# Splitting a weight tile's products into a high pass and a low pass, and mLSTM gates as products

## The chip, the cores and the metric

One Trainium2 chip, one of its cores. The metric is device time in microseconds (us) of one execution. The kernel before takes 2247.6 us (median of 3 runs, 2247.15 to 2248.94).

## What is computed

Four transformer layers over 256 tokens of width 1024, all in float32: two layers of a first kind (with 256 context tokens beside), then two of a second kind. Cut to what matters here:

```
# first kind: h and hc are adaptive RMS norms of x and ctx
q,k,v,gates,o,z, bq,bk,bv,bz, cu,cz, mg = split(h @ w_in)      # 1024 x 13328
h_a = mlstm(q, k, v, gates)          # forward and backward in time
y_a = rmsnorm(h_a) * sigmoid(o) * silu(z)
y_b = diff_attention(bq, bk, bv) * silu(bz);  y_c = fft2(cu) * silu(cz)
x  += gate * ((g_a*(y_a@w_a) + g_b*(y_b@w_b) + g_c*(y_c@w_c)) @ w_out)
# mlstm gates, per head and direction:
b = cumsum(log_sigmoid(f));  m = running max of (b_t - b_s + i_s), carried over chunks
decay weights = exp(b_t - b_s + i_s - m_t);  floor of the denominator = exp(-m_t)
# second kind
x += gt1 * ((sigmoid(ga)*swa(h)@w_o1 + sigmoid(gb)*moba(h)@w_o2) @ w_out)
x += gt2 * (relu(h2 @ w_up)**2 @ w_down)
```

Nearly all arithmetic is in the products with the weight matrices, each of 1024 rows or more.

## The kernel before

**Products in three parts.** A float32 number is split into a high part that TensorE multiplies in one pass (type fp32r) and a low part, the rest. A product of activations A = H + L with weights W = h + l is the sum of three matmuls: H with h, H with l and L with h. The activations' parts are made once, at each norm. The weights' parts are made tile by tile: a tile of 128 x 1024 numbers (512 KB) comes by DMA into a buffer `w`, ScalarE (ACT) copies it with rounding into another (the high part `h`), and VectorE (DVE) subtracts that from the raw tile into a third (the low part `l`). There are 9 such buffers, and some more for a while. Weights are moving data in the form `tok` (activations stand still), and stand still in the form `feat`.

**One program, written by a planner.** `Stream.execute` walks through all weight products in order (`gemm` lists them). For a product it visits pairs (q, o): weight tile q, output o, each output one PSUM bank `mm`. A tile of the usual width 512 holds two slices (`kq` = 2), so a visit is six matmuls: per slice the three parts one after another. After each three matmuls it calls `dma` (next tile's transfer), up to six steps of other work (`plan.side`: attention, norms, gates, evacuations of PSUM, written as generators), and `split` once. These decide where an instruction stands by the planner's own clock; on the chip each engine runs its instructions in the order written.

`split` makes a low part if one is owed and its high part is done by that clock, otherwise the next high part. `tile(i)` is what a visit calls first: it forces both parts of tile i into the program.

```
i = st["base"][q]
h, l = self.tile(i)
for j in range(kq):
    ...
    for m, (L, R, O) in enumerate(outs[o](h[:, s], l[:, s], kt, ps[o])):
        nc.tensor.matmul(O, L, R, ...)
```

The first tiles (`head`) and the last ones (`tail`) of some products are visited output by output, the others tile by tile.

**Gates.** `mlstm_gates` runs once in each of the two layers of the first kind, as side work. On rows (heads on partitions 0 to 3 forward, 32 to 35 backward; time along the row) it makes the sums `b` and maxima `cm`, the four chunks' carries (`TG`, `M`, `off`), and from these four rows per chunk, `R0` and R0 plus three offsets (`r1`, `r2`, `r3`), plus `F`. Five transposes per chunk of 128 time steps turn them into columns `cols`. The other work on TensorE, float32 matmuls and transposes into banks `p0` to `p3`, is written between the weight products; these groups are called p groups below.

Of the kernel before, what the change touches and what calls it, by code (L numbers as in the profile page):

```python
# [49 lines left out]
NSIDE, SLACK, MAXEV, LATE = 6, 1200.0, 4, 400  # L50
NP, NJ, MP = 3, 5, 2
# [284 lines left out]
class Stream:  # L336
# [64 lines left out]
    def build_seq(self):  # L401
# [29 lines left out]
        self.nd = self.ns = self.nl = self.pairs = 0  # L431
# [20 lines left out]
    def split(self, force=False):  # L452
# [5 lines left out]
        if self.nl < self.ns:  # L458
            i = self.gidx[self.nl]
            if force or plan.gate([self.h[i]]) <= plan.t[PE]:  # L460
                r, l = self.raw.pop(i), self.alloc(F32R)
                nc.vector.tensor_tensor(l, r, self.h[i].bitcast(F32), ALU.subtract)
                self.drop(r)
                self.l[i] = l
                self.nl += 1
                return True
        if self.ns < len(self.gidx) and self.pairs < (NP + MP if self.more else NP) and len(self.free) > 1 + self.ns - self.nl:
# [10 lines left out]
    def tile(self, i):  # L478

        plan = self.plan  # L480
        while i not in self.l:
# [10 lines left out]
        late = plan.gate([self.h[i], self.l[i]])  # L492
# [5 lines left out]
        return self.h[i], self.l[i]  # L498

    def execute(self):  # L500
        plan, nc = self.plan, self.nc
        self.build_seq()
        nout, evs = 0, []
# [15 lines left out]
        for st in self.prog:  # L519
# [14 lines left out]
            left = [no] * nq  # L534
            ps, seen = [None] * no, [0] * no
            for q, o in visits:
# [7 lines left out]
                h, l = self.tile(i)  # L544
# [6 lines left out]
                for j in range(kq):  # L551
                    kt = q * kq + j
                    s = slice(j * st["width"], (j + 1) * st["width"])
                    for m, (L, R, O) in enumerate(outs[o](h[:, s], l[:, s], kt, ps[o])):
                        nc.tensor.matmul(O, L, R, start=(kt == 0 and m == 0), stop=(seen[o] == st["nkt"] - 1 and m == 2))
                    seen[o] += 1
                    if j == kq - 1:
                        left[q] -= 1
                        if not left[q]:
                            self.drop(self.h.pop(i))  # L560
                            self.drop(self.l.pop(i))
                            self.pairs -= 1
                            if self.joint and self.joint[0] == i:
                                self.joint.pop(0)
                        if seen[o] == st["nkt"]:
                            evac(st["cb"], o, ps[o])
                    self.dma()
                    n = 0
                    while n < NSIDE and plan.side():
                        n += 1  # L570
                    self.split()
# [11 lines left out]
def _build(tc, a, out, es):  # L583
# [377 lines left out]
    def tok(act, t, c0=0, c1=512):  # L961
        ts = slice(128 * t, 128 * t + 128)

        def f(h, l, kt, ps):
            H, L = act(kt)
            O = ps[:, 0:c1 - c0]
            return [(H[:, ts], h[:, c0:c1], O), (H[:, ts], l[:, c0:c1], O), (L[:, ts], h[:, c0:c1], O)]
        return f

    def feat(view, f0, n):  # L970
        fs = slice(128 * f0, 128 * f0 + 128)

        def f(h, l, kt, ps):
# [4 lines left out]
            return [(h[:, fs], H, O), (h[:, fs], L, O), (l[:, fs], H, O)]  # L978
# [90 lines left out]
    def mlstm_gates(rowt, l, res):  # L1069

        def gen(lane):
            pre, lf, b, v, cm, r1, r2, r3 = (rowt[:, i, :] for i in range(8))
            R = slice(0, 36)
            nc.gpsimd.memset(rowt[R, 2, :], 0.0)
            nc.gpsimd.memset(rowt[R, 4:8, :], 0.0)
# [24 lines left out]
            TG = sm.tile([128, 2, 4], F32, name="TG", tag="TG")  # L1100
            nc.vector.memset(TG, 0.0)
            for i, arr in enumerate((b, cm)):
                fw = arr[0:4].rearrange("p (c n) -> p c n", n=128)[:, :, 127]
                bw = arr[32:36].rearrange("p (c n) -> p c n", n=128)[:, :, 0]
                nc.vector.tensor_copy(TG[0:4, i, 0:2], fw[:, 1:3])
                nc.vector.tensor_copy(TG[0:4, i, 2:4], fw[:, 0:4:3])
                for p, j in POS_B.items():
                    nc.vector.tensor_copy(TG[32:36, i, j:j + 1], bw[:, p:p + 1])
            M = sm.tile([128, 4], F32, name="M", tag="M")
            nc.vector.memset(M, 0.0)  # L1110
            for j in range(3):
                nc.vector.tensor_tensor(M[R, j + 1:j + 2], M[R, j:j + 1], TG[R, 1, j:j + 1], ALU.max)
                nc.vector.tensor_tensor(M[R, j + 1:j + 2], M[R, j + 1:j + 2], TG[R, 0, j:j + 1], ALU.add)
            off = sm.tile([128, 4, 4], F32, name="off", tag="off")
            nc.vector.tensor_copy(off[R, 1, 1:4], TG[R, 0, 0:3])
            nc.vector.tensor_tensor(off[R, 2, 2:4], off[R, 1, 2:4], TG[R, 0, 0:2], ALU.add)
            nc.vector.tensor_tensor(off[R, 3, 3:4], off[R, 2, 3:4], TG[R, 0, 0:1], ALU.add)
            yield [DVE]
            dirs = ((slice(0, 4), POS_F), (slice(32, 36), POS_B))
# [10 lines left out]
            rk = (R0, r1, r2, r3)  # L1130
            nc.gpsimd.memset(r1[R], 0.0)
            for k in (1, 2, 3):
                for rr, pos in dirs:
                    for p, j in pos.items():
                        if j >= k:
                            cs = slice(128 * p, 128 * p + 128)
# [291 lines left out]
    def layer1(l, X, norm, ada_next, begin_out, on_token):  # L1428
# [38 lines left out]
        def g_out(h, lo, kt, ps):  # L1467
            H, L = act(kt)
            return [(h, H, ps), (h, L, ps), (lo, H, ps)]
# [566 lines left out]
    def attend_items(kind, qk, vv, oo, scol, need):  # L2036


        def group(t, p0):
# [4 lines left out]
            def gen(lane):  # L2044
# [36 lines left out]
                for e in range(2):  # L2081
                    for i in range(hpb):
                        if i % 2 == 0 and (e or i):
                            yield []
# [401 lines left out]
```

## Time and profile before

| what | value |
|---|---|
| median of 3 runs | 2247.6 us |
| the profiled execution | 2247.62 us, of it the span 2245.5 us |
| TensorE (PE) busy | 2200.1 us, 98% of the span |
| VectorE (DVE), ScalarE (ACT) busy | 1485.1 us (66%), 1104.3 us (49%) |
| GpSimd (POOL) busy | 272.6 us (12%) |
| DMA | 359.73 MB, mean 160 GB/s |
| granted TensorE clock, mean | 0.997 |

The span runs from the first to the last instruction; 2.1 us of the execution lie around it. Matmuls overlap, and the profile models where each ends, so "busy" is an upper bound of work: a short wait that falls into the modelled end of the matmul before is not shown as idle time.

### The profile page before, as it was taken

What the parts mean: (1) busy time and instruction counts of PE and PEld (TensorE: products, weight loads), DVE (VectorE), ACT (ScalarE), POOL (GpSimd) and SP (SyncE); (2) the same over time, 40 slices, a digit from 0 to 9 for tenths busy, and PEclk for the clock granted to TensorE, in tenths of its full rate; (3) what the DMA queues carried; (4) which work ended last, traced back from release to release, by engine and by line L of the source; (5) the groups of instructions that cost most, each with busy time, mean ns of one, the idle gap of its engine ahead of it and who ended that gap; (6) DMA issues with size and microseconds to landing.
All of it is one profiled execution on the core that took longest, in us unless ns stands there. A gap on an engine that the chain in (4) does not pass through costs nothing. (4 is left out here: it accounts for less than half of the span.)

```text
span 2245.5 us, 33046 instructions
## 1 busy us (share of the span) xinstructions
PE 2200.1 (98%) x12312; PEld 1821.8 (81%) x12312; DVE 1485.1 (66%) x2778; ACT 1104.3 (49%) x2110; POOL 272.6 (12%) x467
## 2 busy tenths in 40 slices
PE   8999999999999999999999999999999999999999
PEld 6877888877777877877778888787898987798987
DVE  4667745457676744687886788677766656758554
ACT  4345422235565522344543466555855645666653
POOL 1013000014121000110200142003000002100000
PEclk9999999999999999999999999999999999999999
DMA  7443344353322453365675423464354564345454
GB/s 297 144 157 109 121 167 140 132 170 118 103 98 96 140 179 131 140 206 187 233 246 185 158 83 135 157 213 151 123 195 165 180 215 160 132 145 203 160 188 150
DMA packets 99905, 359.73 MB, mean 160 GB/s; under 512 B 11960, under 2 KB 12272, under 8 KB 99744
## 3 DMA queue, kind: packets, MB, share of 16 engines
q1 hardware_dynamic: 96192, 348.34, 45.3%
q0 software_dynamic: 3552, 9.28, 1.5%
q8 instruction: 97, 1.59, 0.3%
q14 instruction: 64, 0.52, 0.1%
HBM read 354.37 MB, written 3.20 MB: 159 GB/s over the span
## 5 line engine op out<-in xcount | busy, mean ns | idle before, releaser
L318 DVE TENSOR_TENSOR w<-w,w 128x1024 fp32r<-128x1024 f32 x451 | 551.5, 1223 | 394.0 <-ACT w L318 340.0
L318 ACT ACTIVATE w<-w 128x1024 fp32r<-128x1024 f32 x459 | 485.1, 1058 | 647.6 <-PE mm L318 595.4
L318 PE MATMUL mm<-h,w 128*128 128x256 f32 (+1 forms) x3280 | 665.5, 326 | 2.8 <-DVE w L318 2.3
L318 PE MATMUL mm<-w,h 128*128 128x512 f32 (+1 forms) x1972 | 597.7, 394 | 12.2 <-DVE w L318 9.0
L318 PEld LDWEIGHTS mm<-h,w 128*128 128x128 f32 x3280 | 479.6, 190 | 57.3 <-issue 9.6
L318 PEld LDWEIGHTS mm<-w,h 128*128 128x128 f32 x1972 | 357.2, 190 | 101.4 <-DVE w L318 15.5
L318 PE MATMUL mm<-w,s 128*128 128x512 f32 x1280 | 309.1, 392 | 1.2 <-DVE w L318 1.1
L318 PE MATMUL mm<-w,hl 128*128 128x512 f32 (+1 forms) x800 | 306.7, 383 | 0.0
L318 PEld LDWEIGHTS mm<-w,s 128*128 128x128 f32 x1280 | 238.4, 188 | 52.6 <-DVE w L318 3.2
L318 PE MATMUL mm<-hl,w 128*128 128x512 f32 (+1 forms) x656 | 245.8, 375 | 0.0
L318 PE MATMUL mm<-s,w 128*128 128x512 f32 (+1 forms) x960 | 182.2, 349 | 0.0
L318 PEld LDWEIGHTS mm<-w,hl 128*128 128x128 f32 x800 | 150.8, 189 | 29.9 <-DVE hl L318 0.2
L318 PEld LDWEIGHTS mm<-s,w 128*128 128x128 f32 x960 | 153.1, 190 | 23.5 <-issue 2.0
L318 DVE SCALAR_TENSOR_TENSOR acc<-w,stat,acc 128x512 f32<-128x512 f32 x192 | 143.8, 749 | 42.3 <-DMA w<-in_wada_dram 35.5
L318 PEld LDWEIGHTS mm<-hl,w 128*128 128x128 f32 x656 | 124.0, 189 | 18.7 <-issue 1.0
L318 ACT ACTIVATE s<-mm 128x512 f32<-128x512 f32 (+2 forms) x126 | 65.2, 521 | 62.8 <-PE mm L318 62.8
L318 POOL TENSOR_TENSOR qrs<-qrs,mhalf 128x8 f32<-128x8 f32 (+2 forms) x48 | 77.1, 1607 | 4.0
L318 PE MATMUL p<-s 64*128 64x256 f32 (+3 forms) x464 | 75.4, 389 | 1.4 <-DVE s L318 0.7
L318 POOL TENSOR_SCALAR ls<-ls 128x1 f32<-128x1 f32 x72 | 29.8, 414 | 344.5 <-ACT l1a L318 127.1
L318 PE MATMUL mm<-s,s 128*128 128x512 f32 x256 | 68.7, 390 | 0.0
L318 DVE TENSOR_REDUCE ls<-p 128x1 f32<-128x512 f32 (+1 forms) x96 | 52.8, 595 | 12.7 <-PE p L318 12.3
L318 ACT ACTIVATE s<-w 128x1024 fp32r<-128x1024 f32 x43 | 45.5, 1058 | 27.7 <-PE mm L318 21.0
(348 smaller groups left out, 2399.3 us busy)
## 6 DMA issues: line engine op xcount, KB each, us to landing
w<-in_win_dram SPq DMA_DIRECT2D x272, 512.0 KB, 3.3
w<-in_wada_dram SPq DMA_DIRECT2D x144, 512.0 KB, 3.5
w<-in_wmix_dram SPq DMA_DIRECT2D x64, 512.0 KB, 3.3
w<-in_wup_dram SPq DMA_DIRECT2D x64, 512.0 KB, 3.4
w<-in_wdn_dram SPq DMA_DIRECT2D x64, 512.0 KB, 3.2
w<-in_wo_dram SPq DMA_DIRECT2D x16, 512.0 KB, 3.2
w<-in_wout_dram SPq DMA_DIRECT2D x16, 512.0 KB, 3.5
s<-in_x_dram SPq DMA_DIRECT2D x4, 512.0 KB, 7.3
```

Of the source, the lines that this page charges most:

```text
L318: r = f(*a, **k)
```

## The change

Four edits.

1. **Order of products.** A visit is now a step (q, o, parts). For a middle tile of width 512 (neither the first nor the last tile of its product, nor in `head` or `tail`) the steps go part by part: high x high for all outputs, then the activations' low part with the weights' high part for all outputs, and last the weights' low part for all outputs. For the first tile of a product and for `head` tiles the order within an output is parts 0, 2, 1, where 2 is the weights' low part; for the others 0, 1, 2. Within a step the two slices of one part stand next to each other. (`tok` and `feat` list their parts so that number 2 always holds `l`.)
2. **Splits.** `tile(i)` asks for the high part only unless part 2 is due. `split` prefers a high part while fewer than `AHEAD` = 2 tiles from the current one on have theirs, and the new `pump` (after each three matmuls) may call `split` twice then.
3. **Gates.** Chunk carries are copied with fewer, strided instructions; the maximum with the carry is one instruction for all chunks (before 8). The rows r1, r2, r3 (12 instructions) go; instead four DVE products make offsets times the identity (`off`, 36x144), and two float32 matmuls per chunk add R0 (stationary) times the identity four times and ones times `off`. One transpose (for `F`) stays.
4. In the attention of the second kind of layers a `yield []` becomes `yield [ACT]`.

The core of the diff:

```diff
-        if self.nl < self.ns:
+        if self.nl < self.ns and not (self.ns < self.cur + AHEAD and self.split_high(force)):
...
+    def pump(self):
+        self.dma()
+        if self.ns < self.cur + AHEAD:
+            self.split()
+        n = 0
+        while n < NSIDE and self.plan.side():
+            n += 1
+        self.split()
...
-            visits = [(q, o) for o in range(no) for q in range(hd)]
-            visits += [(q, o) for q in range(hd, nq - tl) for o in range(no)]
-            visits += [(q, o) for o in range(no) for q in range(nq - tl, nq)]
+            early, late = (0, 2, 1), (0, 1, 2)
+            steps = [(q, o, early) for o in range(no) for q in range(hd)]
+            for q in range(hd, nq - tl):
+                if 0 < q < nq - 1 and kq == 2:
+                    steps += [(q, o, (p,)) for p in late for o in range(no)]
+                else:
+                    steps += [(q, o, late if q else early) for o in range(no)]
+            steps += [(q, o, late) for o in range(no) for q in range(nq - tl, nq)]
...
+                for p in parts:
+                    l = self.tile(i)[1] if p == 2 else None
...
+                        L, R, O = outs[o](h[:, s], None if l is None else l[:, s], kt, ps[o])[p]
+                        nc.tensor.matmul(O, L, R, start=(seen[o] == 0), stop=(seen[o] == total - 1))
...
-            for rr, pos in dirs:
-                for p, j in pos.items():
-                    cs = slice(128 * p, 128 * p + 128)
-                    nc.vector.tensor_scalar(cm[rr, cs], cm[rr, cs], M[rr, j:j + 1], None, ALU.max)
+            nc.vector.tensor_tensor(cm4, cm4, MP[R, :, 0:1].to_broadcast([36, 4, 128]), ALU.max)
...
-                            nc.vector.tensor_scalar(rk[k][rr, cs], R0[rr, cs], off[rr, k, j:j + 1], None, ALU.add)
...
+                nc.vector.tensor_tensor(off[:, c], ident[R, R].unsqueeze(1).to_broadcast([36, 4, 36]),
+                                        MP[R, c, 1:5].unsqueeze(2).to_broadcast([36, 4, 36]), ALU.mult)
...
-                for i, arr in enumerate((R0, r1, r2, r3, F)):
-                    nc.tensor.transpose(ps[:, 36 * i:36 * i + 36], arr[R, 128 * p:128 * p + 128], ident[R, R])
+                nc.tensor.matmul(pk, R0[R, cs], ident[R, R].unsqueeze(1).to_broadcast([36, 4, 36]), start=True, stop=False)
+                nc.tensor.matmul(pk, ones[R], off[:, p], start=False, stop=True)
+                nc.tensor.transpose(ps[:, 144:180], F[R, cs], ident[R, R])
```

First place: TensorE, the third tile (q = 2) of the second layer's product `gemm(W(3), ...)`, which makes the second half of the mLSTM values; four outputs. Before, its high part is `w2_8907` and its low part `w8_8944`; `h_7967` and `hl_7968` are the activations' high and low parts, and the `p` rows are the gates' transposes.

```order
L318 MATMUL mm_8889<-w4_8854,hl_7968 128x512
L318 MATMUL mm_8856<-w2_8907,h_7967 128x512
L318 MATMUL mm_8856<-w8_8944,h_7967 128x512
L318 MATMUL mm_8856<-w2_8907,hl_7968 128x512
L318 MATMUL mm_8856<-w2_8907,h_7967 128x512
L318 MATMUL mm_8856<-w8_8944,h_7967 128x512
L318 MATMUL mm_8856<-w2_8907,hl_7968 128x512
L318 MATMUL p2_8963<-cst_80,s3_8624 128x36 x5
L318 MATMUL mm_8869<-w2_8907,h_7967 128x512
L318 MATMUL mm_8869<-w8_8944,h_7967 128x512
```

In the changed program the same tile's high part is `w7_8863` and its low part `w2_8893`, the tile before it `w0_8808` and `w4_8817`:

```order
L319 MATMUL mm_8849<-w4_8817,h_7936 128x512 x2
L319 MATMUL p3_8911<-cst_80,s3_8592 128x144
L319 MATMUL p3_8911<-s3_8592,one_84 128x144
L319 MATMUL p3_8911<-cst_80,s3_8592 128x36
L319 MATMUL mm_8810<-w7_8863,h_7936 128x512 x2
L319 MATMUL mm_8827<-w7_8863,h_7936 128x512
L319 MATMUL p2_8922<-cst_80,s3_8592 128x144
L319 MATMUL p2_8922<-s3_8592,one_84 128x144
L319 MATMUL p2_8922<-cst_80,s3_8592 128x36
L319 MATMUL mm_8827<-w7_8863,h_7936 128x512
L319 MATMUL mm_8835<-w7_8863,h_7936 128x512 x2
L319 MATMUL mm_8849<-w7_8863,h_7936 128x512 x2
```

The low part was read by the tile's second matmul; now eight matmuls with the high part stand first, then eight with `hl_7936` and the high part, and only then those with `w2_8893`. Five transposes of 36 columns have become two products of 144 columns and one transpose.

Second place: VectorE, from the low part of that product's second tile (first row) to the low part of its third (`w8_8944`), with the gates between (`s3` holds the gates' rows, `M` and `off` the carries, `acc` an accumulation for the adaptive norms).

```order
L318 TENSOR_TENSOR w0_8867<-w3_8664,w4_8854 128x1024
L318 TENSOR_SCALAR acc_8866<-w7_8796,stat_88 128x512
L318 SCALAR_TENSOR_TENSOR acc_8866<-w7_8796,stat_88,acc_8866 128x512
L318 TENSOR_SCALAR s3_8624<-s3_8624,M_8839 4x128 x8
L318 TENSOR_TENSOR s3_8624<-s3_8624 36x512
L318 TENSOR_SCALAR s3_8624<-s3_8624 36x512
L318 TENSOR_SCALAR s3_8624<-s3_8624,off_8847 4x128 x12
L318 SCALAR_TENSOR_TENSOR acc_8866<-w7_8887,stat_88,acc_8866 128x512
L318 TENSOR_TENSOR w8_8944<-w5_8702,w2_8907 128x1024
```

The same stretch of VectorE in the changed program, up to the same tile's low part (`w2_8893`):

```order
L319 TENSOR_TENSOR w4_8817<-w8_8629,w0_8808 128x1024
L319 TENSOR_TENSOR modA1_8623<-p2_8815,col_82 128x4
L319 SCALAR_TENSOR_TENSOR modA1_8623<-modA1_8623,col_82 128x4
L319 TENSOR_SCALAR acc_8826<-w2_8761,stat_88 128x512
L319 SCALAR_TENSOR_TENSOR acc_8826<-w2_8761,stat_88,acc_8826 128x512
L319 COPY s3_8592<-s3_8592 4x10
L319 COPY s3_8592<-s3_8592 4x2x5 x3
L319 TENSOR_TENSOR s3_8592<-s3_8592 36x512 x2
L319 TENSOR_SCALAR s3_8592<-s3_8592 36x512
L319 TENSOR_TENSOR s3_8592<-cst_80,s3_8592 36x144 x4
L319 SCALAR_TENSOR_TENSOR acc_8826<-w2_8840,stat_88,acc_8826 128x512 x2
L319 TENSOR_TENSOR w2_8893<-w6_8670,w7_8863 128x1024
```

The 8 and the 12 instructions on 4x128 have gone; four copies, one maximum over 36x512 and four products of 36x144 stand in their place.

## Rows read from the trace of the kernel before

**Rows 1.** The page: span, busiest engine, and the granted clock in 40 slices.
```profile
span 2245.5 us, 33046 instructions
...
PE 2200.1 (98%) x12312; PEld 1821.8 (81%) x12312; DVE 1485.1 (66%) x2778; ACT 1104.3 (49%) x2110; POOL 272.6 (12%) x467
...
PEclk9999999999999999999999999999999999999999
```
**Rows 2.** Waits of PE: total us, times, longest.
```profile
PE mm L318 <- DVE w L318: 12.4, 14, 1.6
...
PE mm L318 <- ACT h L318: 2.7, 3, 1.2
PE mm L318 <- DVE h L318: 2.7, 4, 1.0
...
PE p L318 <- DVE qr L318: 1.7, 2, 1.4
```
**Rows 3.** Timeline of PE, 1017 to 1024 us: start, us, instruction, idle before.
```profile
1019.08 0.39 PE L318 MATMUL mm<-w,hl 128*128 128x512 f32 x1
1019.31 0.39 PE L318 MATMUL mm<-w,h 128*128 128x512 f32 x1
1021.27 0.50 PE L318 MATMUL mm<-w,h 128*128 128x512 f32 x1 [1.58 <-DVE w L318]
1021.62 0.40 PE L318 MATMUL mm<-w,hl 128*128 128x512 f32 x1
...
1022.65 0.50 PE L318 MATMUL p<-cst,s 36*128 36x36 f32 x5
1023.08 0.73 PE L318 MATMUL mm<-w,h 128*128 128x512 f32 x2
```
**Rows 4.** Timeline of DVE, 1008 to 1021.5 us.
```profile
1013.36 1.87 DVE L318 TENSOR_SCALAR s<-s,M 4x128 f32<-4x128 f32 x8
1015.27 0.68 DVE L318 TENSOR_TENSOR s<-s 36x512 f32<-36x512 f32 x1
...
1016.40 2.90 DVE L318 TENSOR_SCALAR s<-s,off 4x128 f32<-4x128 f32 x12
1019.33 0.75 DVE L318 SCALAR_TENSOR_TENSOR acc<-w,stat,acc 128x512 f32<-128x512 f32 x1
1020.00 1.22 DVE L318 TENSOR_TENSOR w<-w,w 128x1024 fp32r<-128x1024 f32 x1
```
**Rows 5.** Timelines of PE at 957.5, 1975, 31 and 1947.5 us.
```profile
959.48 0.50 PE L318 MATMUL mm<-w,h 128*128 128x512 f32 x1 [1.08 <-DVE w L318]
...
1975.98 1.21 PE L318 MATMUL mm<-h,w 128*128 128x256 f32 x8 [1.02 <-DVE w L318]
...
31.67 0.50 PE L318 MATMUL mm<-w,h 128*128 128x512 f32 x1 [0.43 <-DVE w L318]
...
1948.31 0.86 PE L318 MATMUL mm<-h,w 128*128 128x256 f32 x5 [0.47 <-DVE w L318]
```
**Rows 6.** Timeline of PE, 1936.5 to 1943.5 us.
```profile
1937.66 0.63 PE L318 MATMUL p<-cst,qr 128*128 128x128 f32 x4 [1.36 <-DVE qr L318]
1938.05 0.47 PE L318 MATMUL mm<-w,h 128*128 128x512 f32 x1
1940.04 3.91 PE L318 MATMUL mm<-w,h 128*128 128x512 f32 x9 [1.51 <-DVE w L318]
```
**Rows 7.** Windows: us, PE, PEld, DVE, ACT, POOL busy (count), granted clock, DMA.
```profile
1936.00:1939.50 3.50, 1.16 (x7) 0.58 (x5) 3.46 (x7) 3.04 (x10) 1.64 (x1) 1.00 0.42 152
1939.50:1942.90 3.40, 2.87 (x7) 2.30 (x8) 3.40 (x7) 1.28 (x4) 0.00 (x0) 0.63 0.00 0
```
**Rows 8.** The page, groups: busy us, mean ns of one, idle before and releaser.
```profile
L318 DVE TENSOR_TENSOR w<-w,w 128x1024 fp32r<-128x1024 f32 x451 | 551.5, 1223 | 394.0 <-ACT w L318 340.0
L318 ACT ACTIVATE w<-w 128x1024 fp32r<-128x1024 f32 x459 | 485.1, 1058 | 647.6 <-PE mm L318 595.4
```
**Rows 9.** Groups of PE by form: the small float32 products (two records each) and transposes.
```profile
L318 PE MATMUL p<-s,l0b 128*128 128x256 f32 x64 | 15.4, 381 | 0.0
...
L318 PE MATMUL p<-s,l2b 128*128 128x128 f32 x96 | 12.9, 277 | 0.2 <-ACT l2b L318 0.2
...
L318 PE MATMUL p<-cst,s 36*128 36x36 f32 x40 | 4.0, 231 | 0.0
```
**Rows 10.** The page, DMA issues: count, size, us from issue to landing.
```profile
w<-in_win_dram SPq DMA_DIRECT2D x272, 512.0 KB, 3.3
```

More of the change, by code (lines that the diff above doesn't have):

```diff
@@ L476, in split, with high, tile @@
         return False
-    def tile(self, i):
+    def high(self, i):
+        return self.tile(i, False)[0]
+    def tile(self, i, low=True):
         plan = self.plan
-        while i not in self.l:
+        while i not in (self.l if low else self.h):
             self.dma()
@@ L491, in tile @@
                 plan.side(force=True)
-        late = plan.gate([self.h[i], self.l[i]])
+        late = plan.gate([self.h[i], self.l[i]] if low else [self.h[i]])
         while late > plan.t[PE] + LATE:
@@ L502, in execute @@
         self.build_seq()
-        nout, evs = 0, []
+        nout, evs, since = 0, [], 0
         def evac(cb, o, ps):
@@ L543, in execute @@
                 i = st["base"][q]
-                h, l = self.tile(i)
+                self.cur = max(self.cur, self.rank[i])
+                h = self.high(i)
                 if ps[o] is None:
@@ L550, in execute @@
                     nout += 1
[L551 to L571, printed above, removed]
+                for p in parts:
+                    l = self.tile(i)[1] if p == 2 else None
+                    for j in range(kq):
+                        kt = q * kq + j
+                        s = slice(j * st["width"], (j + 1) * st["width"])
+                        L, R, O = outs[o](h[:, s], None if l is None else l[:, s], kt, ps[o])[p]
+                        nc.tensor.matmul(O, L, R, start=(seen[o] == 0), stop=(seen[o] == total - 1))
+                        seen[o] += 1
+                        since += 1
+                        if since >= 3 and seen[o] < total:
+                            since = 0
+                            self.pump()
+                    left[q] -= 1
+                    if not left[q]:
+                        self.drop(self.h.pop(i))
+                        self.drop(self.l.pop(i))
+                        self.pairs -= 1
+                        if self.joint and self.joint[0] == i:
+                            self.joint.pop(0)
+                if seen[o] == total:
+                    evac(st["cb"], o, ps[o])
+                    since = 0
+                    self.pump()
         plan.drain("ev")
@@ L966, in f @@
             O = ps[:, 0:c1 - c0]
-            return [(H[:, ts], h[:, c0:c1], O), (H[:, ts], l[:, c0:c1], O), (L[:, ts], h[:, c0:c1], O)]
+            return [(H[:, ts], h[:, c0:c1], O), (L[:, ts], h[:, c0:c1], O), l is not None and (H[:, ts], l[:, c0:c1], O)]
         return f
@@ L977, in f @@
                 O = O.rearrange("p (t c) -> p t c", c=128)
-            return [(h[:, fs], H, O), (h[:, fs], L, O), (l[:, fs], H, O)]
+            return [(h[:, fs], H, O), (h[:, fs], L, O), l is not None and (l[:, fs], H, O)]
         return f
@@ L1117, in gen @@
[L1117 to L1123 removed]
+            TG, MO, MP = (rowt[:, 7, 128 + o:128 + o + n] for o, n in ((0, 8), (8, 20), (28, 20)))
@@ new lines, in gen @@
+            yield [DVE]
+            by = lambda r, c: MO[r, :, c].rearrange("p k j -> p j k")
+            f_, b_ = slice(0, 4), slice(32, 36)
+            nc.vector.tensor_copy(MP[f_, 1:3, :], by(f_, slice(0, 2)))
+            nc.vector.tensor_copy(MP[f_, 0:4:3, :], by(f_, slice(2, 4)))
+            nc.vector.tensor_copy(MP[b_, 2:0:-1, :], by(b_, slice(0, 2)))
+            nc.vector.tensor_copy(MP[b_, 3::-3, :], by(b_, slice(2, 4)))
+            yield [DVE]
+            cm4 = cm[R].rearrange("p (c n) -> p c n", c=4)
@@ L1124, in gen @@
+            nc.vector.tensor_tensor(cm4, cm4, MP[R, :, 0:1].to_broadcast([36, 4, 128]), ALU.max)
+            yield [DVE]
             F = lf
@@ L1468, in g_out @@
             H, L = act(kt)
-            return [(h, H, ps), (h, L, ps), (lo, H, ps)]
+            return [(h, H, ps), (h, L, ps), lo is not None and (lo, H, ps)]
         def ev_q(f, ps):
@@ L2083, in gen @@
                         if i % 2 == 0 and (e or i):
-                            yield []
+                            yield [ACT]
                         g = slice(2 * i + e, 2 * i + e + 1)
```

59 lines of the change are left out of this document (29 added, 30 removed).

## The prediction

> **What bounds the kernel now.** I read the page first: TensorE is busy 2200.1 of 2245.5 us and its clock is full in every slice [rows 1]. So there are two ways to a shorter time, fewer or shorter matmuls, or less of the 45.4 us in which TensorE is shown idle. The change leaves every weight product as it is, so only the idle time and the small float32 work can move. Then I read who TensorE waits for [rows 2]. The largest item is 12.4 us in 14 waits of weight products for `w` from VectorE, that is for the low part of a weight tile. Waits for activations (2.7 and 2.7 us) and many small ones of the p groups are the rest.
>
> What one such wait costs is seen in the timeline [rows 3]. Products of 512 columns start 0.227 us apart (1019.08 to 1019.31). The next starts at 1021.27, so 1.96 us after, a loss of 1.73, though the idle time shown is 1.58: the modelled end of the matmul before hides 0.15. The one behind starts 0.35 later (1021.62), which is 0.12 more than usual. So each wait costs its idle time and 0.27 us. Fourteen waits: 12.4 + 3.8 = 16.2 us.
>
> Why the low part is late: VectorE makes it in 1.22 us, after ScalarE's 1.06 us for the high part [rows 8], and in the old order the second matmul of a tile already reads it. I matched the 14 waits with the program's order. For each of some 460 tiles I counted the matmul time that is written on TensorE between the low part's instruction and its first reader. In 9 tiles that lead is under 0.3 us; eight of them are eight of the 14 waits, from 959.48 to 1975.98 us, 8.0 us idle together (first and last in [rows 5]; 1940.04 of [rows 6] is one). One wait is the gates' (1021.27, lead 2.3 us). The other five, from 31.67 to 1948.31 us, with 2.8 us, have leads of 0.45 to 1.1 us (first and last in [rows 5]). Of tiles with more lead than 1.3 us only the gates' one waits visibly. So the lead tells the waits.
>
> **The change, part by part.**
>
> *Order of products and earlier high parts.* In a middle tile with four outputs the low part is first read by the 17th matmul, not by the second: 16 x 0.227 = 3.6 us later, longer than the 1.06 + 1.22 us that both parts take. First and last tiles of a product, and all tiles of `head` and `tail`, gain little: there the low part is read third or fifth. Counted in the same way, the changed program has 2 tiles with a lead under 0.3 us (before 9), and 13 between 0.3 and 1.3 us (before 20). Under 2 us there are 33, before 141.
> - The tightest: eight waits cost 8.0 + 8 x 0.27 = 10.2 us; with 2 of 9 left, 7.9 us go.
> - The five others cost 2.8 + 1.4 = 4.1 us; 13 of 20 left, so 1.4 us go.
>
> *The gates on VectorE.* In front of the late low part stand 8 instructions in 1.87 and 12 in 2.90 us [rows 4]. In their place come one maximum over 36x512 (0.68, the row of that size) and four products of 36x144, not shown by the trace: between 0.24 each (2.90/12, 4x128) and 0.68 (36x512); nearest to the short one, I take 0.27, so 1.1 us. Four copies at 0.24 or less add 1.0. VectorE gets 2.0 us back or more just there. The low part began at 1020.00 and takes 1.22, and TensorE wanted it at 1019.54; it had to begin 1.7 us earlier. With the new order it is also read 16 matmuls into its tile. This wait goes: 1.85 us.
>
> *A dip of the clock.* Around 1937 to 1940 us TensorE waits twice (1.36 and 1.51 us), and in the next products the spacing is (3.91 - 0.50)/8 = 0.43 instead of 0.227 us [rows 6], while the granted clock is 0.63 in the mean from 1939.5 to 1942.9 [rows 7]: TensorE runs at its lower level, 1.2 GHz, for most of that stretch, after 1.16 us busy in the 3.5 us before. Eight products at +0.2 are 1.6 us. One of the two waits is a low part with no lead. If it goes, the dip may go; the other wait stays (VectorE busy 3.46 of 3.50 us there). I take half, 0.8 us; ends 0 and 1.6.
>
> *The gates on TensorE.* Eight chunks in all. Five transposes of 36 columns take 0.50 busy (4.0/40 each, [rows 9]). Two products of 144 columns are not in the trace: a float32 product has two records, so one of 128 columns takes 2 x 12.9/96 = 0.27 and one of 256 takes 2 x 15.4/64 = 0.48 us; by width 0.30 each. With the transpose that stays, 0.70. So +0.2 x 8 = 1.6 us. Ends: 0 (if they overlap with their neighbours as the five transposes do, 0.43 from 1022.65 to 1023.08 [rows 3]) and 8 x (2 x 0.48 + 0.10 - 0.43) = 4.2.
>
> *More p groups.* Weight products and p groups alternate in 406 groups, before 387 (counted in the order). Behind a group the next two products take 0.73 instead of 0.62 us [rows 3], so a group costs at most 0.12: 0 to 2.3 us for 19. I take 0.5, because the five transposes ahead took less than their busy time.
>
> *At nothing:* the activations' low part now comes last in `head` tiles, where TensorE waits for activations (5.4 us of [rows 2]); two matmuls more of cover are 0.45 us each, so 0 to 2 us gained; I take 0. Raw tiles stay longer in their buffers, but the leads from a transfer's issue to its high part are the same in both programs in all but a few tiles (over 5 us in 19 of 20, where landing takes 3.3 [rows 10]). `yield [ACT]` lets exponentials wait for ScalarE's clock of the planner; ScalarE is busy half the span [rows 1]. If this cover is gone, the p groups pay, as in the second rival.
>
> Sum, against the profiled execution, 2247.62 us (span 2245.5 and 2.1 around it; the median of the runs is the same, 2247.6): -7.9 - 1.4 - 1.85 - 0.8 + 1.6 + 0.5 = -9.9. **2237.8 us.**
>
> **Rivals.** A measurement of this kernel can tell about 0.2%, 4.5 us, from no change.
>
> 1. *All waits go.* If the 13 short leads cost nothing, 16.2 + 1.6 - 2.1 = 15.7 us are gained: 2231.9; with 2 us from the heads and no price for gates and groups, 2228. For it: of the twenty with short leads before, only five waited visibly. Chance 0.15.
>
> 2. *The other side: ScalarE serves the high parts first.* `split` may now run twice in a `pump`, high parts first, and each keeps ScalarE 1.06 us [rows 8] ahead of an attention step's exponential or evacuation, which the p group behind it waits for. Place: the attention stretches, as at 1937, where the engines around TensorE are full [rows 7]. Price 1.06 us for each p group that is late by one copy. From 10 of them on the gain is eaten, from 14 on it is slower by more than 0.2%; with 18, 2237.8 + 19.1 = 2256.9. Against it: the p groups' leads, counted as above, have the same spread in both programs (106 and 107 under 1 us), and high parts are not more, only earlier. Chance 0.08.
>
> 3. *The wait only moves.* VectorE sits idle 340.0 us before low parts because ScalarE's high part isn't there [rows 8]. If high parts are late for reasons that the order doesn't change (their buffer is freed by TensorE: ScalarE's 595.4 us, [rows 8]), the first matmul of a tile waits in place of the second, and only the prices remain: 2247.6 + 2.1 = 2249.7; with half of the gain 2243. Against it: now no weight product waits visibly for ScalarE's `w`; [rows 2] have only `h` from there. Chance 0.15.
>
> 4. *Going round the banks.* TensorE now changes its PSUM bank after every two products in middle tiles, before after six. In the trace a change of bank costs nothing: 1019.08 to 1019.31 is one, at the usual 0.227 [rows 3]. If it made TensorE pause often, the clock would dip as at 1939.5, at 1.6 us each; from 6 dips on the gain is gone, from 9 on it is slower. With 15: 2261.8. The Trainium skill says so of one kernel (page "TensorE: Matmul & The Clock Gate", section "A second HAM failure mode: psum-queue depth-cycling"): cycling through banks made TensorE idle briefly between groups so often that its clock oscillated. By that rule this change would lose; this trace has bank changes every six products and a full clock [rows 1], so it does not bear the rule out so far. Chance 0.03.
>
> **The numbers.** The likeliest case has 0.59, with its own range 2231 to 2244 (ends of the dip, of the gates' products and the groups). The range that should hold 8 in 10, 2228 to 2246, takes in the first rival and half of the third, and leaves out the second, the fourth and the rest of the third, 0.18. Faster by over 0.2%: 0.56 + 0.15 = 0.71. Within: 0.03 + 0.15 = 0.18, with 0.01 of the second 0.19. Slower: 0.07 + 0.03 = 0.10.
>
> **What would show it.** In the waits of TensorE after, `mm` for `w` from VectorE falls from 12.4 us to 4 or less, and no new line `mm` for `w` from ScalarE comes up beyond 1 us (rival 3). The p lines together stay within 3 us (rival 2). The spacing of 512-wide products stays 0.227 where banks change, and the clock has no more dips than before (rival 4). The gates' VectorE stretch is 2 us or more shorter, and the wait behind it is gone. The products of 144 columns take about 0.3 us. I would be wrong most likely in how many of the short leads that remain turn into waits, since those sit in first and last tiles where the new order helps least, and in waits of p groups, which any new interleaving moves.

## The result, and the profile after

The changed kernel takes 2235.6 us (median of 4 runs, 2232.4 to 2236.7), the kernel before in the same session 2247.4 us (4 runs, 2246.0 to 2248.9): ratio 0.9945, 95% interval 0.9928 to 0.9962. It is faster by 11.8 us; 9.9 were forecast.

The page of after, with the span, the engines and the granted clock in 40 slices:

```profile
span 2233.0 us, 33003 instructions
...
PE 2197.6 (98%) x12312; PEld 1822.4 (82%) x12312; DVE 1479.2 (66%) x2738; ACT 1104.2 (49%) x2110; POOL 262.5 (12%) x465
...
PEclk9999999999999999999999999999999999999999
```

Beside [rows 1] the span is 12.5 us shorter and TensorE is busy 2.5 us less, so 10.0 of the 12.5 us are idle time. The waits of PE in after:

```profile
PE mm L319 <- DVE w L319: 4.8, 8, 1.1
PE mm L319 <- ACT h L319: 4.2, 4, 1.7
PE mm L319 <- DVE s L319: 2.9, 4, 1.2
PE mm L319 <- ACT s L319: 2.6, 3, 1.4
PE p L319 <- ACT l1a L319: 1.8, 1, 1.8
```

The waits for low parts are 4.8 us in 8 where [rows 2] have 12.4 in 14. The weight products' waits for activations (`h` and `s`, on either engine) are 10.1 us in all, before 6.5. The p groups' waits, without those for the adaptive norms' weights by DMA, are 8.0 us, before 12.7. These sums are over all lines of that view. The first is read off one line; the other two are easily missed, since they are spread over many.

The groups that stood in [rows 8], now of after:

```profile
L319 DVE TENSOR_TENSOR w<-w,w 128x1024 fp32r<-128x1024 f32 x450 | 549.8, 1222 | 348.1 <-ACT w L319 234.8 <-PE mm L319 72.2 <-PE p L319 30.6
L319 ACT ACTIVATE w<-w 128x1024 fp32r<-128x1024 f32 x462 | 488.1, 1058 | 540.0 <-PE mm L319 487.9 <-DVE w L319 14.9 <-issue 14.6
```

VectorE's idle time ahead of low parts that ScalarE ends fell from 340.0 to 234.8 us. This is the new order of products, and not the early high parts: with `AHEAD = 0` (below) it is 249.0 us, and with `AHEAD = 2` in the old order 341.2. The timeline of PE where [rows 3] show the gates:

```profile
1014.30 1.98 PE L319 MATMUL mm<-w,h 128*128 128x512 f32 x8
1016.12 1.98 PE L319 MATMUL mm<-w,hl 128*128 128x512 f32 x8
1017.93 0.61 PE L319 MATMUL mm<-w,h 128*128 128x512 f32 x2
1019.13 0.48 PE L319 MATMUL p<-cst,s 36*128 36x144 f32 x2 [0.58 <-DVE s L319]
1019.45 0.41 PE L319 MATMUL p<-s,one 36*128 36x144 f32 x2
1019.69 0.19 PE L319 MATMUL p<-cst,s 36*128 36x36 f32 x1
1019.82 0.50 PE L319 MATMUL mm<-w,h 128*128 128x512 f32 x1
```

Eight products with the high part, over four banks, start (1016.12 - 1014.30)/8 = 0.2275 us apart, as products did before: a change of bank every two products costs nothing here. The wait of 1.58 us for a low part is gone, and one of 0.58 us for the gates' rows has come. A chunk's gates now take 1019.82 - 1019.13 = 0.69 us, before 1023.08 - 1022.65 = 0.43. VectorE's part of them, which [rows 4] show before:

```profile
1016.72 0.48 DVE L319 COPY s<-s 4x10 f32<-4x10 f32 x4
1017.24 1.40 DVE L319 TENSOR_TENSOR s<-s 36x512 f32<-36x512 f32 x2
1018.57 0.41 DVE L319 TENSOR_SCALAR s<-s 36x512 f32<-36x512 f32 x1
1018.91 0.95 DVE L319 TENSOR_TENSOR s<-cst,s 36x144 f32<-36x144 f32 x4
```

From 1016.72 to 1019.86 it takes 3.1 us, before from 1013.36 to 1019.30 5.9. One product of 36x144 takes 0.24 us. And windows of after at the place of [rows 7] and at a new place (us, PE, PEld, DVE, ACT, POOL busy, granted clock, DMA):

```profile
1937.00:1940.50 3.50, 3.50 (x32) 3.50 (x31) 2.15 (x5) 2.22 (x6) 0.00 (x0) 1.00 0.61 167
...
1311.50:1315.00 3.50, 2.46 (x19) 2.02 (x17) 2.90 (x8) 2.19 (x7) 0.24 (x1) 1.00 0.48 150
1315.00:1319.00 4.00, 3.26 (x11) 1.86 (x13) 3.55 (x9) 2.47 (x6) 0.78 (x3) 0.66 0.00 0
```

The dip of the clock at 1940 us is gone, and one of the same kind has come at 1316 us, behind the wait of 1.8 us for `l1a`.

Where the gain arises can be read off as well. Every kernel of this case starts 9584 weight products, in the same order of products (but for one swap below, at another place), so the start of the one with a given number can be compared. From the 3600th to the 4440th, behind the gates of the second layer, and from the 7560th to the 8160th, around 1940 us, the windows are (matmuls into `mm` alone: us, PE busy (count), granted clock, DMA), before and then after:

```profile
1027.10:1253.30 226.20, 195.31 (x840) 1.00 0.59 205
1877.50:2007.20 129.70, 103.19 (x601) 0.99 0.40 136
...
1027.50:1248.25 220.75, 192.60 (x841) 1.00 0.62 211
1872.55:1995.10 122.55, 102.04 (x602) 1.00 0.44 146
```

The first stretch is 5.5 us shorter and the second 7.1 (1.7 us of this is the dip of the clock in the profiled run of before). That is the whole gain: everywhere else gains and losses cancel.

### The profile page after: what moved, and what is told of

Its sections match the earlier page's. It is cut to its first block, busy times and chain, and to the rows that moved or that the text cites. A ratio compares the mean times of both kernels' runs of the same rounds, so it can differ in the third digit from the quotient of the medians.

```text
span 2233.0 us, 33003 instructions
## 1 busy us (share of the span) xinstructions
PE 2197.6 (98%) x12312; PEld 1822.4 (82%) x12312; DVE 1479.2 (66%) x2738; ACT 1104.2 (49%) x2110; POOL 262.5 (12%) x465
## 5 line engine op out<-in xcount | busy, mean ns | idle before, releaser
L319 DVE TENSOR_TENSOR w<-w,w 128x1024 fp32r<-128x1024 f32 x450 | 549.8, 1222 | 348.1 <-ACT w L319 234.8
L319 PE MATMUL mm<-h,w 128*128 128x256 f32 (+1 forms) x3264 | 582.9, 325 | 2.5 <-DVE w L319 1.5
L319 PE MATMUL mm<-w,h 128*128 128x512 f32 (+1 forms) x2020 | 529.6, 388 | 7.7 <-ACT h L319 4.2
L319 PEld LDWEIGHTS mm<-h,w 128*128 128x128 f32 x3264 | 468.5, 190 | 51.9 <-issue 7.2
L319 PE MATMUL mm<-w,s 128*128 128x512 f32 x1276 | 298.0, 391 | 1.4 <-ACT s L319 1.4
L319 PE MATMUL mm<-w,hl 128*128 128x512 f32 (+1 forms) x800 | 234.3, 388 | 0.0
L319 PE MATMUL mm<-hl,w 128*128 128x512 f32 (+1 forms) x656 | 183.9, 383 | 0.0
L319 PEld LDWEIGHTS mm<-hl,w 128*128 128x128 f32 x656 | 118.0, 188 | 26.0 <-issue 5.5
L319 PE MATMUL mm<-s,s 128*128 128x512 f32 x260 | 62.5, 391 | 0.2 <-ACT s L319 0.2
L319 ACT ACTIVATE s<-p 128x512 fp32r<-128x512 f32 (+3 forms) x68 | 35.7, 528 | 54.0 <-PE p L319 54.0
L319 PEld LDWEIGHTS p<-s 64*128 64x128 f32 (+1 forms) x464 | 41.6, 187 | 23.6 <-issue 12.6
```

The lines of the kernel that those rows point to most:

```text
L319: r = f(*a, **k)
```

## The experiments

Twelve more kernels ran. The first question was which edit earns the time. The theory was that the leads of the low parts tell it. The kernel before ran beside them on the same chips: 2246.32 us (29 runs) for the first four, 2246.34 (23) for the next four, 2245.75 (17) for the last.

**Order alone.** The changed kernel with `AHEAD = 0` (which switches the preference and the second call off), the old gates and the old `yield`.

```diff
-AHEAD = 2
+AHEAD = 0
...
-                nc.tensor.matmul(pk, ones[R], off[:, p], start=False, stop=True)
-                nc.tensor.transpose(ps[:, 144:180], F[R, cs], ident[R, R])
+                for i, arr in enumerate((R0, r1, r2, r3, F)):
+                    nc.tensor.transpose(ps[:, 36 * i:36 * i + 36], arr[R, 128 * p:128 * p + 128], ident[R, R])
...
-                            yield [ACT]
+                            yield []
```

> The new order of products alone: high parts are split as before (low first), gates and attention as before. Theory (the lead of the low part tells the waits): tiles with a lead under 0.3 us stay 9, those up to 1.3 us fall from 20 to 10, and the gates' wait goes by the later reading; so 1.85 + 2.0 us and the dip's 0.8 go, some 4 to 5 us: about 2243, and the waits of products for low parts are 7 to 9 us. Rival (the order of products does it all, early high parts nothing): 2236, and those waits fall to 5 us as in the changed kernel.

Measured: 2260.0 us (2256.7 to 2261.6), ratio 1.0053 [1.0034, 1.0073]. Theory and rival both missed: it is slower than before. Waits of PE:

```profile
PE mm L319 <- DVE w L319: 13.0, 13, 2.2
...
PE mm L319 <- ACT w L319: 1.2, 3, 0.5
```

The waits for low parts did not fall, and waits for ScalarE's high parts have come, which the kernel before and the changed kernel don't have.

**Gates alone**, in the kernel before (the gates' part of the diff and nothing else).

> The kernel before with the gates of the changed one alone. Theory: the wait behind the gates (1.85 us) goes, the gates' products cost 1.6 us: 2247.4, within 1.5 us of before. Rival (the gates' lighter VectorE work is a large part of the gain): 2243 or less.

Measured: 2245.6 us (2244.1 to 2248.8), ratio 0.9990 [0.9979, 1.0001]. As expected: the gates' wait is gone (low parts 10.5 us), and the total hardly moves.

**The change without early high parts.**

```diff
-AHEAD = 2
+AHEAD = 0
```

> The changed kernel with AHEAD = 0: order of products, gates and attention as changed, but low parts go first again. Leads under 0.3 us: 6 (2 in the changed kernel), up to 1.3 us: 11 (13). Theory (lead): 4 tight tiles more at 1.3 us each, so about 5 us slower than the changed kernel, 2240 to 2241. Rival (order does it all): the same as the changed kernel, 2235 to 2236.

Measured: 2251.4 us (2249.2 to 2257.5), ratio 1.0018 [1.0007, 1.0029]. The theory misses by 11 us, the rival by more. Most of what is lost goes at one place, in the second layer, ahead of the weight products that make the third unit of the differential attention. They reuse the first unit's buffer (`need` = `b(0)`), so its attention, which is side work, must be done first. Timeline of PE:

```profile
1314.30 0.40 PE L319 MATMUL mm<-h,w 128*128 128x256 f32 x2
1316.09 1.16 PE L319 MATMUL p<-s,l0b 128*128 128x128 f32 x8 [1.40 <-ACT l0b L319]
...
1318.47 0.66 PE L319 MATMUL p<-cst,qr 128*128 128x128 f32 x4 [1.11 <-ACT vb L319]
...
1323.36 2.45 PE L319 MATMUL p<-s 64*128 64x512 f32 x6
...
1333.30 1.18 PE L319 MATMUL mm<-w,h 128*128 128x512 f32 x2
```

and windows of the same place:

```profile
1317.50:1321.00 3.50, 1.49 (x7) 0.74 (x7) 1.95 (x6) 2.68 (x9) 1.02 (x3) 0.95 0.00 0
1321.00:1324.50 3.50, 3.32 (x11) 1.84 (x13) 1.56 (x4) 0.98 (x2) 0.00 (x0) 0.50 0.00 0
1324.50:1328.00 3.50, 3.50 (x15) 2.53 (x14) 2.46 (x7) 2.13 (x7) 0.00 (x0) 0.50 0.00 0
```

From 1314.3 to 1333.3 us there is no further weight product, only 57 matmuls of p groups that had been left over. Several wait for the step before them with no weight product to cover the wait, and the clock then falls to its lower level (0.50, that is 1.2 of 2.4 GHz) for 13.7 us. In after the same place has 7 such matmuls in 3.7 us. From the weight product before this place to the one behind it (1301 to 1346 us), this run loses 11.6 us to the kernel before, after 1.9. In the two stretches where the changed kernel gains 5.5 and 7.1 us, this run gains 3.4 and 4.4 us: the new order earns there without the second edit, and loses more elsewhere.

**Early high parts alone**: the old order with the new `split`, gates and `yield`, and the second call.

```diff
                     self.dma()
+                    if self.ns < self.cur + AHEAD:
+                        self.split()
                     n = 0
                     while n < NSIDE and plan.side():
```

> The kernel before with the order of products as it was, but high parts split ahead (AHEAD = 2) and gates and attention as changed. Leads under 0.3 us: 7 (9 before), up to 1.3 us: 21 (20). Theory (lead): 2 tight tiles fewer, 2.6 us, and 1.85 of the gates less 1.6: about 2245. Rival (early high parts do it all): 2236 to 2238. If instead the early high parts hinder ScalarE's other work: above 2249.

Measured: 2246.2 us (2243.5 to 2250.2), ratio 0.9997 [0.9986, 1.0008]. As expected: no gain. So neither half of the change lowers the total alone, and both together lower it by 11.8 us.

**What are the waits worth?** All products with a weight's low part read the high part instead, so no product depends on VectorE's low part (it is still made). The planner reckons with the operands too: without the low part it writes the other work in another order, so the two programs differ from the kernels they come from by more than the waits (the order of matmuls from 98.8 us on in the kernel before, from 135.4 us on in the changed one).

```diff
-... enumerate(outs[o](h[:, s], l[:, s], kt, ps[o])):
+... enumerate(outs[o](h[:, s], h[:, s], kt, ps[o])):
```

In the kernel before:

> The kernel before, but the products of the weights' low part read the high part instead (the low parts are still made, nobody reads them; the output is then not the reference's). No product waits for a low part. Theory: the 14 waits and the dip of the clock go, 16.2 + 1.6 us: 2229 to 2230. Rival (a wait taken away comes back as another, for high parts or at the drains): 2238 or more.

Measured: 2244.2 us (2241.2 to 2245.9), ratio 0.9988 [0.9979, 0.9996]. Waits of PE:

```profile
PE mm L318 <- DVE h L318: 4.1, 4, 1.0
PE p L318 <- ACT l1a L318: 4.1, 2, 2.4
PE mm L318 <- ACT s L318: 3.1, 3, 1.5
PE p L318 <- DVE l0b L318: 3.0, 3, 1.2
```

No wait for a low part is left, and the time falls by 2.2 us, not by 16: the number is the rival's. The other waits grew from 26.3 to 35.1 us, and half-clock stretches of 6.8 and 10.2 us came, the second at the same place as above (16.5 us without a weight product). With the loss to the clock taken out of all runs (the last column of the table below), the gain is 8.1 us. How much of what came back is due to the waits that went, and how much to the other order of the side work, this run can't tell. The same edit in the changed kernel:

> The changed kernel, but the products of the weights' low part read the high part instead (the low parts are still made, nobody reads them; the output is then not the reference's). Theory: the 8 waits left go, 4.8 + 8 x 0.27 = 7.0 us: 2228 to 2230, the same as the kernel before without these waits, since the order of products then has nothing left to hide. Rival (the order of products has a price of its own, at the drains): 3 us or more above the kernel before without these waits.

Measured: 2237.4 us (2234.1 to 2244.1), ratio 0.9958 [0.9944, 0.9972]. Theory and rival both missed: it is no faster than the changed kernel with its 4.8 us of such waits, and faster than the kernel before without them. Here too the side work is in another order.

**Cover for the leftover work.** In the second layer another product is put ahead of the place where the leftover groups stand.

```diff
-            unit(2, "s3", b(0))
             bz(1)
+            unit(2, "s3", b(0))
```

With `AHEAD = 0`:

> The changed kernel with AHEAD = 0 (2251.4), and in the second layer bz(1), a product that needs no attention, stands before unit(2), which waits until attention heads of unit 0 are done. Theory (the 11.6 us that AHEAD = 0 loses between 1301 and 1346 us are a drain without weight products, and the clock that falls in it): this loss goes, 2240 to 2243, and the granted clock has no stretch of 13.7 us at half. Rival (the new order loses because TensorE changes banks more often): 2250 or more.

Measured: 2257.5 us (2255.1 to 2261.0), ratio 1.0047 [1.0035, 1.0059]. In the changed kernel:

> The changed kernel with bz(1) before unit(2). Theory: the changed kernel loses 1.9 us at the same drain (a wait of 1.8 us and a dip of 3.4 us); these go: 2233 to 2235. Rival: the attention behind is then late at the next drain: 2236 or more.

Measured: 2241.1 us (2234.3 to 2249.4), ratio 0.9976 [0.9963, 0.9989]. Both theories missed, and the times are in the rivals' ranges. The leftover groups only move to the next such place (68 matmuls in 19.6 us at 1397, and 82 in 21.3 us at 1392), with a half-clock stretch of 10.2 us there in both. The first rival's reason, the changes of bank, isn't borne out: the changed kernel has the same order, keeps 0.2275 us across them and takes 2235.6 us. The second kernel has the longest such stretch of all, and yet with the loss to the clock taken out it is only 2.6 us above the changed kernel.

**Which part of the second edit?** `pump` without its extra call of `split`; the preference for high parts stays.

```diff
     def pump(self):
         self.dma()
-        if self.ns < self.cur + AHEAD:
-            self.split()
```

> The changed kernel, but pump calls split once in every case, as before the change; split still prefers high parts while fewer than two tiles are ahead. Theory (the second call of split in a pump, not the preference, is what the new order needs, because with one call per three matmuls high and low parts share one place in the program): the counts of short leads are those of the run without AHEAD (7 under 0.3 us, 11 up to 1.3; there 6 and 11; in the changed kernel 2 and 13), so the time is that run's, 2251 us (2248 to 2254), and span less the time lost to the clock is about 2240. Rival (each new interleaving moves the time by several us and the runs without AHEAD were unlucky): about 2240 us, anywhere from 2234 to 2246, with no relation to that run.

Measured: 2249.7 us (2247.8 to 2253.5), ratio 1.0015 [1.0006, 1.0024]. In the theory's range, and outside the rival's: without the second call the gain is gone. Waits of PE:

```profile
PE mm L319 <- DVE w L319: 8.7, 11, 1.9
PE mm L319 <- DVE s L319: 7.1, 7, 1.7
...
PE p L319 <- DVE s L319: 2.8, 2, 2.5
```

This run has no large leftover (7 matmuls in 3.5 us at the place above, 23 in 6.7 us at 638), so a large leftover is not needed to lose the gain. In the two stretches it gains 3.3 and 4.4 us on the kernel before, as `AHEAD = 0` does, and loses them elsewhere. Against after, weight products wait 5.1 us more for weight parts in 6 more waits (5.1 + 6 x 0.27 = 6.7 us by the prediction's price) and p groups 3.5 us more: 10.2 of the 13.0 us between the two profiled spans.

**More of it**: `AHEAD = 3`.

> The changed kernel with AHEAD = 3 in place of 2. Theory (high parts ahead are what earns the time in the new order): no lead under 0.3 us is left and 8 up to 1.3 us, so it is no slower than the changed kernel: 2235 us (2231 to 2239), span less the time lost to the clock 2225 to 2229. Rival (schedule chance): between 2231 and 2252, above 2240 as likely as not.

Measured: 2255.4 us (2251.7 to 2255.6), ratio 1.0038 [1.0026, 1.0050]. The theory fell: it is slower than the kernel before. Waits of PE:

```profile
PE mm L319 <- ACT h L319: 5.1, 7, 1.7
PE p L319 <- ACT l0a L319: 3.8, 2, 3.5
...
PE p L319 <- DVE ls L319: 3.0, 3, 1.3
PE p L319 <- DVE vb L319: 2.6, 3, 1.0
```

Waits for weight parts are down to 0.4 us, as the leads say. The p groups' waits are 21.7 us, against 8.0 in after, and leftover stretches of 60 matmuls in 15.1 us (at 638 us) and 47 in 15.5 us (at 1323) are back. Half-clock stretches add up to 30.7 us.

**The two remaining edits undone, one at a time.** The old `yield`:

```diff
-                            yield [ACT]
+                            yield []
```

> The changed kernel with the attention's yield [ACT] undone. The program differs only in the attention stretch of the third layer and shortly behind it. Theory (the fourth edit is worth nothing of its own): 2236 us, within 3 us of the changed kernel. Rival (it carries part of the gain, by keeping the p groups from waiting for exponentials): 2240 us or more, with TensorE's waits of p groups for ScalarE 2 us or more above those of the changed kernel.

Measured: 2235.2 us (2232.3 to 2238.5), ratio 0.9953 [0.9940, 0.9966]. The old gates, as in the first experiment:

> The changed kernel with the old gates. Theory (order and AHEAD carry the gain; by the run with the new gates alone the gates give 1 to 2 us net): 2237 us (2234 to 2240), the wait for a low part behind the gates at about 1020 us back with 1 to 2 us or hidden by the 16 matmuls ahead of it. Rival (schedule chance, since all that stands behind the gates is interleaved anew): between 2231 and 2252, above 2241 as likely as not.

Measured: 2235.0 us (2231.2 to 2238.7), ratio 0.9950 [0.9936, 0.9965]; waits of 1.06 us for a high part and 0.50 us for a low part stand at the gates. These kernels are 10.6 and 10.7 us faster than the kernel before beside them, the changed kernel 11.8: neither of the two edits alone is worth anything that can be measured. Both undone together, with `AHEAD = 2`, did not run.

**All runs in one table.** Leads under 0.3 us are counted in the program as in the prediction; waits are sums of the waits of PE (weight parts from VectorE or ScalarE; activations; p groups without DMA); "alone" is the longest run of p groups without a weight product after the first 30 us; "half" the time at the lower clock level in the profiled run, without start and end. The last column is the median over the timed runs of the span times its mean granted clock, that is, the span less what the clock took. The clock is given to 0.001, so 2.2 us, and a wait that falls into a half-clock stretch is taken off by half too.

| kernel | leads < 0.3 | weight parts | activations | p groups | alone | half | median us | at full clock |
|---|---|---|---|---|---|---|---|---|
| before | 9 | 12.4 | 6.5 | 12.7 | 4.1 | 3.4 | 2246 to 2247 | 2238 to 2239 |
| after | 2 | 4.8 | 10.1 | 8.0 | 3.7 | 3.4 | 2235.6 | 2227.0 |
| gates alone | 9 | 10.5 | 6.5 | 13.2 | 4.1 | 0 | 2245.6 | 2239.7 |
| order alone | 9 | 14.2 | 8.7 | 14.1 | 18.9 | 20.5 | 2260.0 | 2245.8 |
| AHEAD 0 | 6 | 8.1 | 8.5 | 13.9 | 18.9 | 17.1 | 2251.4 | 2240.2 |
| AHEAD 0, cover | 6 | 10.2 | 8.3 | 16.4 | 19.6 | 13.7 | 2257.5 | 2244.3 |
| after, cover | 2 | 5.5 | 8.1 | 11.9 | 21.3 | 27.3 | 2241.1 | 2229.6 |
| preference only | 7 | 9.9 | 10.4 | 11.5 | 6.7 | 3.4 | 2249.7 | 2241.5 |
| AHEAD 3 | 0 | 0.4 | 6.6 | 21.7 | 15.5 | 30.7 | 2255.4 | 2235.6 |
| old order, AHEAD 2 | 7 | 9.6 | 6.4 | 12.4 | 4.1 | 0 | 2246.2 | 2241.0 |
| after, old gates | 2 | 8.1 | 9.8 | 7.1 | 3.9 | 10.2 | 2235.0 | 2226.5 |
| after, old yield | 1 | 3.8 | 10.0 | 7.7 | 4.2 | 17.1 | 2235.2 | 2225.5 |
| before, low part unread | - | 0 | 9.0 | 19.8 | 16.5 | 17.1 | 2244.2 | 2230.3 |
| after, low part unread | - | 0 | 12.7 | 14.2 | 6.2 | 13.7 | 2237.4 | 2230.0 |

The leads go with the waits for weight parts through the whole column (9 and 10.5 to 14.2, 6 or 7 and 8 to 10, 1 or 2 and 4 to 8, none and 0.4). They don't tell the time: `AHEAD = 3` has next to no such wait and takes 2255.4 us. Of the programs with the new order whose products read the low parts, the four with the second call and `AHEAD = 2` take 2225.5 to 2229.6 us at full clock, the four without it 2240.2 to 2245.8. So at full clock the second call goes with more than 10 us.

## Why the prediction was right, and where it was not

The time and the sign were right, and the waits for low parts fell nearly as far as forecast. Between the two profiled spans (12.5 us) the terms measure so:

- **Low parts** (-7.9 and -1.4, with the gates' wait -1.85: -11.15). The visible waits for them fell by 7.6 us and 6 in number, by the prediction's own price 7.6 + 6 x 0.27 = 9.2 us. "4 or less" was forecast, 4.8 is left. The step that isn't borne out is the price: "each wait costs its idle time and 0.27 us", taken as what the whole program gains when the wait goes. The kernel before with no such wait gained 2.2 us, or 8.1 at full clock, where the price gives 16.2, and has other waits and half-clock stretches in their place. Since its side work stands in another order, how much of the price the program gets back is not shown. At the wait itself the price is borne out: where a product of 512 columns waits behind another in after, 0.16 to 0.17 us of the wait is not shown as idle and the next product starts 0.11 us late (11 waits).
- **p groups** (+0.5). Wrong in sign: their waits fell by 4.7 us. In the run without the second call of `split` they wait 3.5 us more than in after, so that call may have the larger part in this. Which of the moved instructions does it was not isolated.
- **Heads** ("at nothing", 0 to 2 us gained): outside the bounds. Waits for activations rose by 3.6 us. The prediction counted the two matmuls that stand in between, and not that TensorE gets there earlier; this last is argued, not shown.
- **Gates.** VectorE got 2.8 us back (2.0 forecast), the wait for the low part behind is gone (one of 0.58 us for the gates' rows stands there now), and a product of 144 columns takes 0.295 us (32 records, 0.1475 us apart in the mean; 0.30 forecast). TensorE's part is 8 x (0.69 - 0.43) = 2.1 us, where +1.6 was taken; the upper end given for it, 4.2, should read 8 x 0.63 = 5.0. The net, -0.25 in the forecast, is nothing that can be measured: the gates alone are 0.7 us faster, and the changed kernel without them gains 10.7 us in place of 11.8.
- **The dip at 1940** (-0.8). It went, and one of the same length came at 1316 us: 0. The half-clock stretch in the first 20 us is 3.4 us in the profiled run of after and 6.8 in that of before; this gives 1.7 us and was not forecast.

The sum: -9.2 - 4.7 + 3.6 + 2.1 - 1.7, and 0.6 us less for the adaptive norms' DMA, is -10.5 of the -12.5; 2.0 stay without a place. So the near hit is in part luck: the term for low parts was 2 us too large, p groups brought 5 us that were not forecast, and the heads took 3.6 back.

Another step fell. The prediction treated early high parts as one more way to longer leads. With the leads of `AHEAD = 0` (6 and 11 against 2 and 13) it gives 2240 us, and 2251 were measured. In the two stretches where the changed kernel gains, each of the programs with the new order gains on the kernel before (1.3 to 6.5 us in the first, 2.2 to 7.4 in the second with the dip's 1.7, one profiled execution each), with the second edit or without; old order and early high parts give -1.1 and 2.1. So the new order earns there, and the second edit keeps it from losing as much elsewhere. What it loses without that edit has two shapes: side work that is put off until it stands alone where a product needs it (`AHEAD = 0`), or more and longer waits with no such stretch (the preference alone).

Of the rivals, the second (weight parts go first on ScalarE and p groups pay) is not what this change does. Its sign is seen with `AHEAD = 3`: p waits of 21.7 us and a time 9.6 us above before. Its place there is the leftover work ahead of a product, and not the attention stretch at 1937 that the prediction named; that the high parts on ScalarE cause it is not shown. The third (the wait moves to ScalarE's `w`) isn't seen in after, which has no such line, but the new order without the second edit has it in part: 1.2 us in 3 waits. The fourth is not seen: products keep 0.2275 us across a change of bank every two, and the granted clock is 0.9 or more in each of the 40 slices of after. The Trainium skill's page "TensorE: Matmul & The Clock Gate", section "A second HAM failure mode: psum-queue depth-cycling", tells of a kernel in which cycling through banks made the clock oscillate. By the spacing and the clock just given, this trace does not show that.

Open: by which waits the second call earns that, and why a third tile ahead loses it. The planner's clock decides where the side work lands, and every edit moves all that is written behind it; nine programs of the new order don't tell a rule from this program's chance.

## What to carry to other kernels

The idle time that a profile puts down to one producer need not be what its removal earns: other waits can take its place. Letting the consumer read something that is there already is a cheap test, but in a program that a planner writes, see first whether the order of instructions stayed the same. Undo each edit alone and run each alone; here two edits that earn nothing or lose apart earn 0.5% together, and each of two others could be undone without a measurable loss. Compare the start of the nth main product in both traces: it shows where a gain arises, and where it is lost again. Where work beside the main stream is put off, look for the place where it is collected; here such stretches lasted up to 21.3 us, with up to 13.7 us at the lower clock.

## What the runs showed of the hardware

In the profiled runs the clock's lower level comes in stretches of 3.4 to 13.7 us behind waits, and not in every execution of the same instructions. The changed kernel and the one with the old `yield` have the same first 8042 of 12312 matmuls, up to 1580 us. Behind the gates at about 1018 us the one waits 0.58 us and keeps its clock (1.00 in the window 1018 to 1022). The other waits 1.08 us, and its windows there read:

```profile
1014.00:1018.00 4.00, 3.02 (x14) 2.17 (x12) 3.38 (x10) 0.35 (x1) 0.29 (x1) 1.00 0.32 112
1018.00:1022.00 4.00, 3.90 (x16) 2.56 (x16) 3.73 (x11) 2.18 (x3) 0.00 (x0) 0.78 0.41 159
1022.00:1026.00 4.00, 4.00 (x13) 2.96 (x13) 1.56 (x5) 0.00 (x0) 0.00 (x0) 0.50 0.40 134
```

The stretch lasts 10.2 us and costs half of that. The same place took 13.7 us at the lower level in the profiled run of the changed kernel with cover (its windows behind the gates):

```profile
1014.00:1017.00 3.00, 1.67 (x9) 1.08 (x7) 2.92 (x10) 0.52 (x1) 0.00 (x0) 1.00 0.45 141
1017.00:1024.00 7.00, 7.00 (x24) 4.88 (x24) 4.67 (x13) 2.00 (x3) 0.00 (x0) 0.58 0.47 164
1024.00:1031.00 7.00, 7.00 (x19) 5.21 (x18) 2.22 (x5) 0.00 (x0) 0.00 (x0) 0.50 0.24 75
```

Twelve runs of that kernel spread over 2234.3 to 2249.4 us with mean clocks of 0.991 to 0.999. So a few half-clock stretches, which differ from execution to execution, are as large as the effect that this case is about, and a single profile can't tell two such kernels apart.
